# Three FFNs norm ahead of their products; 18 of 22 column tiles of w1 go in pairs by seven half-depth products

## The chip, the cores and the metric

One program runs on one core of one Trainium2 chip. The time is the device time of one execution in microseconds; before the change the median of three runs was 3161.38 us (3160.10 to 3161.64). The engines are named as in the profile: PE is TensorE, DVE VectorE, ACT ScalarE, POOL GpSimd, SP the queue that issues most DMAs.

## The reference

An encoder trunk of two layers for 512 prompt tokens and 32 sample tokens (544 together), width 1024, FFN width 2816. Only the FFNs are touched; `mixing` stands for a large projection, four branches and an output product.

```python
def rms_norm(x, g):
    y = x * lax.rsqrt(jnp.mean(x * x, axis=-1, keepdims=True) + EPS)
    return y * g
def swiglu(x, w1, w3, w2):
    return (jax.nn.silu(x @ w1) * (x @ w3)) @ w2
def layer(...):
    x = x + 0.5 * swiglu(rms_norm(x, n1), f1a, f1b, f1c)      # FFN1
    x = x + mixing(rms_norm(x, nm), ...)
    x = x + 0.5 * swiglu(rms_norm(x, n2), f2a, f2b, f2c)      # FFN2
    x = x + sigmoid(rms_norm(x, npl) @ wpg) * (p_i @ wpp)     # ple
```

All of it is in fp32.

## The kernel before

**Layout.** Activations lie with features on the partitions: `x` is eight tiles of 128 x 544. The tokens go in two halves `h` of 272 (`HT`). A product for one column tile of 128 weights and one half runs over the depth in steps of 128, and each step is three matmuls (`mm`, L344): the weight's high part with the activation's high part (`nh`, `ah`), high with the activation's low part (`nl`, `al`), low with the high part. High and low are two fp32r tiles which sum to the fp32 value.

**Weights.** The order of all products is planned ahead. `Weights.load` issues DMAs on SP into three raw tiles of 8 x 128 x 128; `split_next` casts the next job's raw tile to `hi` on ACT (L129) and leaves `lo = raw - hi` on DVE (L133) to be emitted after the cast of the next job (`late`, `finish`). Six tiles of each kind are live at most.

**Order.** The program is written as a sequence of units. `unit(fn)` splits one weight tile (`W.pump`), then emits the DVE work that earlier units put off (`settle` empties the list that `later` fills), then the unit itself, then a step of a side chain (`tick`). Each engine does its own list in that order; there is no scheduler. Products go to four PSUM banks in turn (`pm()`); four others serve statistics and side chains (`ps1()`).

**FFN.** `ffn` takes the 22 column tiles in parts of 8, 8 and 6 (`FF_PARTS`). For each tile f and half h, w1's product and w3's product are made; r is the token's factor rsqrt(mean(x^2)). DVE scales w1's product by r (`u`, L403), ACT makes tanh(u/2) (L297), DVE (tanh+1)*u (L306), w3's product times r (L403) and the product of both (L512), then ACT and DVE split it into `ah` (L323) and `al` (L321). After a part's tiles the d phase multiplies by w2 with the depth of that part and adds to x (L526), 16 units (m, h).

**Norms.** `Norm.update` runs as each x tile becomes final: hi and lo of x times gain (L370, L371), the square (L383), its sum on POOL. The two statistics matmuls (L392) stand inside the first unit of the next stage, behind its first product (`middle`), and r is applied to products only. `run_tail` emits the last product of the stage before. `p_chain` is a side chain for the per-layer embedding; it is started ahead of FFN2.

Of the kernel before, what the change touches and what calls it, by code (L numbers as in the profile page):

```python
# [27 lines left out]
FF_PARTS = ((0, 8), (8, 8), (16, 6))  # L28
OFF = dict(xp=0, q=512, k=1024, v=1536, gu=2048, gv=2560, lq=3072, lk=3328, lv=3584,
# [4 lines left out]
RAW_BUFS, W_BUFS, S_BUFS, T_BUFS = 3, 6, 57, 14  # L34
# [39 lines left out]
class Weights:  # L74

    def __init__(self, nc, raw_p, w_p):
        self.nc, self.raw_p, self.w_p = nc, raw_p, w_p
        self.chunks, self.jobs = [], []  # L80
        self.n_dma = self.n_split = self.live = 0
        self.raw_live = 0
        self.late = None

    def chunk(self, src, k0, nk, n0, ncols):

        step = max(1, 1024 // (nk * 128)) * 128
        hs = []
        for c in range(0, ncols, step):
            w = min(step, ncols - c)  # L90
            ck = dict(src=src, k0=k0, nk=nk, n0=n0 + c, n=w, left=1, raw=None, queued=False)
            job = dict(ck=ck, c=0, w=w, uses=2 * max(1, w // 128), hi=None, lo=None, queued=False)
            hs += [(job, o) for o in range(0, w, 128)]
        return hs

    def order(self, h):
        job = h[0]
        if not job["queued"]:
            job["queued"] = True
            self.jobs.append(job)  # L100
            if not job["ck"]["queued"]:
                job["ck"]["queued"] = True
                self.chunks.append(job["ck"])
# [10 lines left out]

    def split_next(self, lower=None):
        job = self.jobs[self.n_split]
        self.n_split += 1
        ck = job["ck"]
        while ck["raw"] is None:
            self.load()  # L120
        w = job["w"]
        if w < 128:
            both = self.w_p.tile([128, ck["nk"], 2 * w], F32R, tag="hi", name="hi")
            hi, lo = both[:, :, 0:w], both[:, :, w:2 * w]
        else:
            both = hi = self.w_p.tile([128, ck["nk"], w], F32R, tag="hi", name="hi")
            lo = self.w_p.tile([128, ck["nk"], w], F32R, tag="lo", name="lo")
# [14 lines left out]
        self.live += 1  # L142
# [7 lines left out]
    def pump(self, n=1):  # L150
        self.load()
        for _ in range(n):
            if self.n_split < len(self.jobs) and self.live < W_BUFS:
                self.split_next()

    def get(self, h):
        job, o = h
        while job["hi"] is None:
            assert self.live < W_BUFS, "weight slots"
# [13 lines left out]
def tile_encoder_step(ctx: ExitStack, tc: tile.TileContext, a, outs):  # L173
# [249 lines left out]
    for L in range(DEPTH):  # L423
        pl = {}

        def ffn_plan(key, w1, w3, w2):
            p1, p3, p2 = [], [], []
            for (f0, nf) in FF_PARTS:
                for f in range(f0, f0 + nf, 2):
                    c1 = W.chunk(w1, 0, 8, f * 128, 256)  # L430
                    c3 = W.chunk(w3, 0, 8, f * 128, 256)
                    p1 += c1
                    p3 += c3
# [22 lines left out]
        ffn_plan("ffn1", a["ffn1_w1"][L], a["ffn1_w3"][L], a["ffn1_w2"][L])  # L456
# [21 lines left out]
        ffn_plan("ffn2", a["ffn2_w1"][L], a["ffn2_w3"][L], a["ffn2_w2"][L])  # L478
# [1035 lines left out]
    with tc.manual_schedule():  # L1514
# [125 lines left out]
```

## Time and profile before

| what | value |
|---|---|
| median of three runs | 3161.38 us |
| the profiled execution | 3162.79 us |
| its span | 3160.8 us |
| mean granted clock of TensorE | 0.997 |
| PE busy | 3123.7 us, 99% |
| DVE busy | 1765.7 us, 56% |
| ACT busy | 1282.7 us, 41% |
| POOL busy | 312.3 us, 10% |

A busy engine is one with an instruction in it; matmuls overlap one another, so the mean length of one is more than the distance from one to the next. The chain of waits goes back from the last instruction to what released each step. The granted clock is a share of full speed: 1.00 is 2.4 GHz and 0.50 is 1.2 GHz.

### The profile page before, as it was taken

To read this page: it belongs to the slowest core of one execution; us is meant where nothing else is said; L and a number is where in the kernel's file an instruction comes from. 1 tells how busy PE (TensorE), PEld (TensorE's weight loads), DVE (VectorE), ACT (ScalarE), POOL (GpSimd) and SP (SyncE) were. 2 spreads that over 40 slices of the span, in tenths; PEclk is the share of its full clock that TensorE was granted. 3 is DMA by queue.
4 is the path that set the end of the run, shared out by engine and by line. 5 is a ranking of instruction groups with operands and counts; after the bars stand their busy time and mean duration, and the time that the engine had idled before them with its cause. 6 is when DMAs were issued, how large, how long until landed. Compare 5 with 4: busy or idle time off the path is not lost.

```text
span 3160.8 us, 58903 instructions
## 1 busy us (share of the span) xinstructions
PE 3123.7 (99%) x24756; PEld 3078.9 (97%) x24756; DVE 1765.7 (56%) x3503; ACT 1282.7 (41%) x2274; POOL 312.3 (10%) x413
## 2 busy tenths in 40 slices
PE   8999999999999999999999999999999999999999
PEld 8999998999999999999999999988999999999999
DVE  6444556866665554545654545477656645535454
ACT  4222334466664342223532223244666634323233
POOL 2000021201122000000300000112101211000010
PEclk9999999999999999999999999999999999999999
DMA  5333242224233323232323232422333232323221
GB/s 148 87 87 92 76 141 75 69 72 156 75 99 109 93 89 90 85 94 75 94 87 94 86 89 82 137 72 64 126 101 109 78 109 87 94 88 89 85 87 63
DMA packets 487337, 295.06 MB, mean 93 GB/s; under 512 B 13654, under 2 KB 472614, under 8 KB 487072
## 3 DMA queue, kind: packets, MB, share of 16 engines
q1 hardware_dynamic: 471392, 248.94, 27.1%
q0 software_dynamic: 11504, 34.55, 3.2%
q10 hardware_dynamic: 4176, 7.80, 0.7%
q8 instruction: 195, 3.19, 0.4%
q14 instruction: 70, 0.57, 0.1%
HBM read 270.41 MB, written 20.83 MB: 92 GB/s over the span
## 4 chain that ended last, share of the span: by engine, by line
PE 95%; DVE 3%; ACT 1%; issue 1%; DMA 0%; ACTq 0%; SPq 0%; DVEq 0%
PE pm L344 87%; DVE qe L828 1%; PE ps L868 1%; PE ps L1329 1%; PE ps L604 1%; PE ps L1320 1%; PE ps L1237 0%; PE ps L334 0%; DVE lo L133 0%; PE ps L1287 0%; PE ps L1286 0%; PE ps L905 0%; PE ps L1214 0%; PE ps L1176 0%; PE pm L707 0%
## 5 line engine op out<-in xcount | busy, mean ns | idle before, releaser
L344 PE MATMUL pm<-nh,hi 128*128 128x272 f32 x5248 | 1527.7, 291 | 0.0
L344 PE MATMUL pm<-nh,lo 128*128 128x272 f32 x5248 | 1512.2, 288 | 2.9 <-DVE lo L133 2.1
L344 PE MATMUL pm<-nl,hi 128*128 128x272 f32 x5248 | 1511.3, 288 | 0.0
L344 PEld LDWEIGHTS pm<-nh,hi 128*128 128x128 f32 x5248 | 989.4, 189 | 8.1 <-issue 5.9
L344 PEld LDWEIGHTS pm<-nh,lo 128*128 128x128 f32 x5248 | 988.1, 188 | 3.6 <-DVE lo L133 2.5
L344 PEld LDWEIGHTS pm<-nl,hi 128*128 128x128 f32 x5248 | 989.5, 189 | 1.2 <-DVE nl L1558 0.2
L129 ACT CAST hi<-raw 128x1024 fp32r<-128x1024 f32 (+2 forms) x478 | 491.0, 1027 | 390.2 <-PE pm L344 357.6
L133 DVE TENSOR_TENSOR lo<-raw,hi 128x1024 fp32r<-128x1024 f32 (+1 forms) x475 | 569.6, 1199 | 2.7 <-ACT hi L129 2.2
L403 DVE TENSOR_TENSOR u<-pm,r 128x272 f32<-128x272 f32 x560 | 246.4, 440 | 507.8 <-PE pm L344 497.7
L344 PE MATMUL pm<-ah,lo 128*128 128x272 f32 x1408 | 405.3, 288 | 0.0
L344 PE MATMUL pm<-al,hi 128*128 128x272 f32 x1408 | 405.2, 288 | 0.0
L344 PE MATMUL pm<-ah,hi 128*128 128x272 f32 x1408 | 405.2, 288 | 0.0
L344 PEld LDWEIGHTS pm<-al,hi 128*128 128x128 f32 x1408 | 265.0, 188 | 0.0
L344 PEld LDWEIGHTS pm<-ah,lo 128*128 128x128 f32 x1408 | 265.0, 188 | 0.0
L344 PEld LDWEIGHTS pm<-ah,hi 128*128 128x128 f32 x1408 | 264.9, 188 | 0.0
L323 ACT CAST ah<-sg 128x272 fp32r<-128x272 f32 x176 | 73.9, 420 | 439.9 <-DVE sg L512 439.9
L385 POOL TENSOR_TENSOR acc<-acc,sq 128x272 f32<-128x272 f32 x84 | 66.2, 789 | 1785.9 <-ACT sq L383 1785.9
L526 DVE SCALAR_TENSOR_TENSOR x<-pm,x 128x272 f32<-128x272 f32 x192 | 84.6, 441 | 270.3 <-PE pm L344 269.8
L297 ACT ACTIVATE sg<-u 128x272 f32<-128x272 f32 x192 | 82.9, 432 | 342.9 <-DVE u L403 342.9
L297 ACT ACTIVATE u<-u 128x272 f32<-128x272 f32 x160 | 69.0, 432 | 218.4 <-DVE u L403 218.2
L344 PE MATMUL pm<-yl,hi 128*128 128x272 f32 x512 | 147.4, 288 | 0.0
L344 PE MATMUL pm<-yh,hi 128*128 128x272 f32 x512 | 147.3, 288 | 0.0
(321 smaller groups left out, 3462.8 us busy)
## 6 DMA issues: line engine op xcount, KB each, us to landing
raw<-in_ffn_w_dram SPq DMA_DIRECT2D x240, 512.0 KB, 3.7
raw<-in_w_in_dram SPq DMA_DIRECT2D x136, 512.0 KB, 3.7
raw<-in_w_branch_dram SPq DMA_DIRECT2D x32, 512.0 KB, 3.4
raw<-in_ffn_w_dram SPq DMA_DIRECT2D x32, 384.0 KB, 3.1
raw<-in_w_out_dram SPq DMA_DIRECT2D x16, 512.0 KB, 3.6
raw<-in_ple_w_gate_dram SPq DMA_DIRECT2D x16, 512.0 KB, 3.5
yp<-park ACTq DMA_DIRECT2D x24, 272.0 KB, 4.5
park<-x POOLq DMA_DIRECT2D x16, 272.0 KB, 7.4
```

The lines of the kernel that those rows point to most:

```text
L129: self.nc.scalar.copy(hi, src)
L133: (lower or self.nc.vector).tensor_tensor(out=lo, in0=src, in1=hi.bitcast(F32), op=ALU.subtract)
L297: nc.scalar.activation(out, x, AF.Tanh, scale=scale)
L323: nc.scalar.copy(hi, src)
L344: nc.tensor.matmul(ps, lhsT=w[:, k, o:o + 128], rhs=x[:, hs(h)], start=first and k == 0 and j == 0, stop=last and k == n - 1 and j == 2)
L385: eng.tensor_tensor(out=self.acc[:, s], in0=self.acc[:, s], in1=q, op=ALU.add)
L403: nc.vector.tensor_tensor(out=out, in0=ps, in1=self.r[:, hs(h)], op=ALU.mult)
L526: nc.vector.scalar_tensor_tensor(out=x[m][:, hs(h)], in0=ps, scalar=0.25, in1=x[m][:, hs(h)], op0=ALU.mult, op1=ALU.add)
L604: nc.tensor.transpose(ps[0:n, g * 128:(g + 1) * 128], s[:, t0:t0 + n], ident)
L828: nc.vector.tensor_tensor(out=q2[r, e_].rearrange("p (b h) -> p b h", h=h), in0=uppers(e3[r, l], h), in1=uppers(qs, h), op=ALU.mult)
L868: nc.tensor.matmul(banks[f][0:n, j * n:(j + 1) * n], lhsT=kk, rhs=qq, start=True, stop=True)
L1320: nc.tensor.matmul(zb[n][:, 0:WID[n]], lhsT=ntri, rhs=sp[n][j][:, 0:WID[n]], start=j == 0, stop=False)
```

## The change

Three of the four FFNs (FFN2 of both layers and FFN1 of layer 1) get their input already normed (`PreNorm`) and run in `ffn7`; FFN1 of layer 0 stays. In `PreNorm` the statistics are taken at the end of the stage before; `normalise` makes y = x*r on DVE, hi = y*gain on ACT and lo on DVE for each x tile and half, and the FFN's products need no factor afterwards.

`ffn7` takes the tiles in parts of 4, 6, 6 and 6. The four tiles of part 0 go as plain products; in `first` three products are made together, step by step over the depth. In the other parts two tiles of w1 by two halves of tokens by two halves of depth are one 2 x 2 product of blocks (Winograd's form of Strassen): seven products of half the depth (12 matmuls each) in place of eight. Its operands are blocks and sums of blocks. Those of the weights (`a22, a11, s1, s3, a12, s2, s4`, `split_operand`) are summed in place in the raw tiles by DVE (L176 of the new kernel), cast by ACT (L179) and completed by DVE (L183); those of the activations (`t1` to `t4`) are made once per FFN by a side chain (`combine`). A pair's seven products, and four whole products of w3, are laid out in seven units (`pair`); products accumulate onto sums that DVE writes into PSUM.

Over the program 24182 matmuls become 23858: 27 pairs with 84 in place of 96. The w2 loads of the eight-deep and six-deep parts become four-deep and six-deep ones of the same bytes in all, 12 more DMAs; each FFN has 16 more updates of x. `p_chain` now starts ahead of the last part's d phase.

```diff
+QUAD = ("a22", "a11", "s1", "s3", "a12", "s2", "s4")
+FF_PARTS7 = ((0, 4), (4, 6), (10, 6), (16, 6))
...
+    def quad(self, src, n0):
+        c0, c1 = [dict(src=src, k0=0, nk=8, n0=n0 + c, n=128, left=1, raw=None, queued=False) for c in (0, 128)]
+        js = {name: dict(cks=[c0, c1] if name[0] == "s" else [(c0, c1)[int(name[1]) - 1]], of=(c0, c1), slots=1, uses=1,
+                         hi=None, lo=None, queued=False, kind=name) for name in QUAD}
+        return {name: (j, 0) for name, j in js.items()}
...
+    def split_operand(self, job):
+        name, (c0, c1) = job["kind"], job["of"]
+        both = self.slot(8, 128)
+        hi, lo = both[:, 0:4], both[:, 4:8]
+        v = self.nc.vector
+        a11, a12, a21, a22 = (c["raw"] and c["raw"][:, e::2, :] for c in (c0, c1) for e in (0, 1))
+        src, add = dict(a11=(a11, None), a12=(a12, None), a22=(a22, None), s1=(a22, a21), s3=(a21, a11),
+                        s2=(a11, a22), s4=(a12, a11))[name]
+        if add is not None:
+            v.tensor_tensor(out=src, in0=src, in1=add, op=ALU.add)
+            if name == "s2":
+                self.done_with(c1)
+        self.nc.scalar.copy(hi, src)
+        self.finish()
+        def low():
+            v.tensor_tensor(out=lo, in0=src, in1=hi.bitcast(F32), op=ALU.subtract)
+            if name == "s4":
+                self.done_with(c0)
+        self.late = (job, low)
+        job["hi"], job["lo"] = hi, lo
...
+    class PreNorm(Norm):
...
+        def normalise(self, h, ks):
+            s = hs(h)
+            low = None
+            for m in ks:
+                if self.out[m] is None:
+                    self.out[m] = (st(f"nh{m}", F32R), st(f"nl{m}", F32R))
+                if self.y[h][m // 2] is None:
+                    self.y[h][m // 2] = st("y")
+                hi, lo = (p[:, s] for p in self.out[m])
+                y, g = self.y[h][m // 2][:, hs(m % 2)], self.gain[:, m:m + 1]
+                nc.vector.tensor_tensor(out=y, in0=self.x[m][:, s], in1=self.r[:, s], op=ALU.mult)
+                nc.scalar.mul(hi, y, g)
+                if low:
+                    low()
+                def low(hi=hi, lo=lo, y=y, g=g):
+                    nc.vector.scalar_tensor_tensor(out=lo, in0=y, scalar=g, in1=hi.bitcast(F32),
+                                                   op0=ALU.mult, op1=ALU.subtract)
+            low()
...
+        def combine(self):
+            self.minus = lay.tile([128, 8], F32, tag="minus", name="minus")
+            nc.vector.tensor_scalar(self.minus, self.gain, -1.0, None, op0=ALU.mult)
+            for j in range(4):
+                g, g2, m2 = self.gain[:, 2 * j:2 * j + 1], self.gain[:, 2 * j + 1:2 * j + 2], \
+                    self.minus[:, 2 * j + 1:2 * j + 2]
+                y1, y2 = self.y[0][j], self.y[1][j]
+                self.y[0][j] = self.y[1][j] = None
+                d = st("yd")
+                nc.vector.tensor_tensor(out=d, in0=y1, in1=y2, op=ALU.subtract)
+                (ha, la), (hb, lb) = self.sums[j] = [(st("sh", F32R), st("sl", F32R)) for _ in range(2)]
+                sa, sb = st("sa"), st("sb")
+                t1 = sa[:, 0:HT]
+                nc.scalar.mul(t1, d[:, 0:HT], g)
+                b12 = tt_("b12")
+                nc.scalar.mul(b12, y2[:, 0:HT], g)
+                yield
...
+                b22 = y2[:, HT:T]
+                stt = nc.vector.scalar_tensor_tensor
+                stt(out=sa[:, HT:T], in0=b22, scalar=m2, in1=t1, op0=ALU.mult, op1=ALU.subtract)
+                nc.scalar.copy(ha, sa)
+                stt(out=sb[:, 0:HT], in0=b22, scalar=g2, in1=b12, op0=ALU.mult, op1=ALU.subtract)
+                stt(out=sb[:, HT:T], in0=d[:, HT:T], scalar=m2, in1=t1, op0=ALU.mult, op1=ALU.add)
+                nc.scalar.copy(hb, sb)
+                yield
...
+        if isinstance(norm, PreNorm):
+            for m, h in order[:-1]:
+                unit(lambda: fn(m, h))
+                if (m, h) == (7, 0):
+                    later(norm.finish)
+            norm.stats(0)
+            W.pump(1)
+            settle()
+            norm.normalise(0, range(0, 2))
+            fn(*order[-1])
+            norm.normalise(0, range(2, 4))
+            norm.finish()
+            tick(1)
+            norm.normalise(0, range(4, 8))
+            return
...
+                    c3 = W.chunk(w3, 0, 8, f * 128, 256)
+                    p3 += c3
+                    if parts is FF_PARTS7 and f0 > 0:
+                        q = W.quad(w1, f * 128)
+                        p1 += [q, None]
+                        for x in [q[n] for n in QUAD[:-1]] + [c3[0], q["s4"], c3[1]]:
+                            W.order(x)
+                        continue
...
+        def other(f, h, t, sign=1.0):
+            ps = pm()
+            mm(ps, p3[f], norm.out, h)
+            later(lambda: half_done(f, h, t, ps, sign))
...
+        def first(h):
+            tiles = [pm(), pm(), pm()]
+            ws = [W.get(x) for x in (p1[0], p3[0], p1[1])]
...
+                if k == 3 and h == 0:
+                    norm.stats(1)
+            for x in (p1[0], p3[0], p1[1]):
+                W.used(x)
+            t = silu(tiles[0])
+            t2 = silu(tiles[2])
+            later(lambda: half_done(0, h, t, tiles[1]))
+            return t2
...
+        def product(ps, w, b, first=True):
+            hi, lo, _ = W.get(w)
+            for j, (xh, xl) in enumerate(norm.block(b)):
+                for i, (u, z) in enumerate(((hi, xh), (hi, xl), (lo, xh))):
+                    nc.tensor.matmul(ps, lhsT=u[:, j, :], rhs=z, start=first and j == 0 and i == 0,
+                                     stop=j == 3 and i == 2, skip_group_check=not first)
+            W.used(w)
...
+            def u1():
+                v["a"], v["e"], v["b"] = pm(), pm(), pm()
+                product(v["a"], q["a11"], "b11")
+                product(v["e"], q["s1"], "t1")
+                product(v["b"], q["s2"], "t2")
+                v["as"], v["es"] = tt_("as"), tt_("es")
+                nc.scalar.copy(v["as"], v["a"])
+                nc.scalar.copy(v["es"], v["e"])
+                def sums():
+                    nc.vector.tensor_tensor(out=v["b"], in0=v["b"], in1=v["as"], op=ALU.add)
+                    nc.vector.tensor_tensor(out=v["e"], in0=v["b"], in1=v["es"], op=ALU.add)
+                later(sums)
+            def u3():
+                product(v["a"], q["a12"], "b21", first=False)
+                v["t11"] = silu(v["a"])
+                later(lambda: half_done(f, 0, v["t11"], v["g"]))
+                product(v["b"], q["s3"], "t3", first=False)
+                product(v["e"], q["s4"], "b22", first=False)
+                def last_one():
+                    c = v["es"]
+                    nc.vector.tensor_tensor(out=c, in0=v["b"], in1=c, op=ALU.add)
+                    v["t22"] = silu(c, -1.0)
+                later(last_one)
+                v["t12"] = silu(v["e"])
+            def u2():
+                v["g"] = pm()
+                mm(v["g"], p3[f], norm.out, 0)
+            def u5():
+                product(v["b"], q["a22"], "t4", first=False)
+                v["t21"] = silu(v["b"], -1.0)
+            unit(u1)
+            unit(u2, pump=2)
+            unit(u3)
+            unit(lambda: other(f, 1, v["t12"]), pump=2)
+            unit(u5)
+            unit(lambda: other(f + 1, 0, v["t21"], -1.0))
+            unit(lambda: other(f + 1, 1, v["t22"], -1.0))
...
+            if part == 0:
+                for h in (0, 1):
+                    settle()
+                    t2 = first(h)
+                    unit(lambda: other(1, h, t2), pump=0)
+                    if h == 0:
+                        norm.normalise(1, range(8))
+                c_sums = start(norm.combine(), front=True)
+                for f in range(2, nf):
+                    for h in (0, 1):
+                        def f_unit():
+                            ps = pm()
+                            mm(ps, p1[f], norm.out, h)
+                            t = silu(ps)
+                            W.pump(1)
+                            other(f, h, t)
+                        unit(f_unit)
+            else:
+                if part == 1:
+                    drain(c_sums)
+                for f in range(f0, f0 + nf, 2):
+                    pair(f)
...
-            ffn(pl["ffn1"], x, norm, nm)
-            n2 = Norm(x, v["norm_ffn2"])
+            (ffn7 if L else ffn)(pl["ffn1"], x, norm, nm)
+            n2 = PreNorm(x, v["norm_ffn2"])
             mixing(L, v, x, nm, n2)
             npl = Norm(x, v["norm_ple"])
             ppair.clear()
-            start(p_chain(L))
-            ffn(pl["ffn2"], x, n2, npl)
+            ffn7(pl["ffn2"], x, n2, npl, p_chain(L))
...
-                norm = Norm(x, vn["norm_ffn1"])
+                norm = PreNorm(x, vn["norm_ffn1"])
```

**A pair's fourth unit.** On ACT, in the first pair of FFN2 of layer 0 (the new kernel), the rows from the cast of `s1` of the next pair (w_14068) on; pm_13990 is the bank `a`, pm_13991 the bank `e`, w_14112 is `s3` of the next pair:

```order
L179 CAST w_14068<-raw_13926 128x512
L343 ACTIVATE sg_14084<-pm_13990 128x272
L343 ACTIVATE sg_14110<-pm_13991 128x272
L179 CAST w_14112<-raw_13926 128x512
L179 CAST w_14116<-raw_13988 128x512
L369 CAST ah_14120<-sg_14084 128x272
L343 ACTIVATE sg_14125<-es_14030 128x272
```

On DVE in the same place:

```order
L176 TENSOR_TENSOR raw_13926<-raw_13926,raw_13988 128x4x128
L183 TENSOR_TENSOR w_14068<-raw_13926,w_14068 128x512
L183 TENSOR_TENSOR w_14112<-raw_13926,w_14112 128x512
L352 SCALAR_TENSOR_TENSOR sg_14084<-sg_14084,pm_13990 128x272
L708 TENSOR_TENSOR sg_14084<-sg_14084,pm_14043 128x272
L778 TENSOR_TENSOR es_14030<-pm_13992,es_14030 128x272
```

and on PE, the last product of the third unit and the first matmuls of the fourth, whose bank pm_14128 is the one that pm_13990 had:

```order
L747 MATMUL pm_13991<-nh5_13104,w_13922 128x272
L747 MATMUL pm_13991<-nh7_13115,w_13922 128x272
L747 MATMUL pm_13991<-nl7_13116,w_13922 128x272
L747 MATMUL pm_13991<-nh7_13115,w_13922 128x272
L390 MATMUL pm_14128<-nh0_13048,hi_13862 128x272
L390 MATMUL pm_14128<-nl0_13049,hi_13862 128x272
```

In the kernel before, on DVE at the end of part 0 of the same FFN, the same steps read:

```order
L321 TENSOR_TENSOR al_15668<-sg_15641,ah_15667 128x272
L403 TENSOR_TENSOR u_15700<-pm_15674,r_13151 128x272
L133 TENSOR_TENSOR lo_15607<-raw_15478,hi_15606 128x1024
L306 SCALAR_TENSOR_TENSOR sg_15702<-sg_15702,u_15700 128x272
L403 TENSOR_TENSOR u_15700<-pm_15675,r_13151 128x272
L512 TENSOR_TENSOR sg_15702<-sg_15702,u_15700 128x272
L133 TENSOR_TENSOR lo_15705<-raw_15576,hi_15704 128x1024
```

DVE's read of the bank (there L403, here L352) stood ahead of the weight tile's lo that the same unit cast; now it stands behind the lo of `s3`, whose cast stands on ACT behind the tanh of `e`.

**Part 0's d phase.** On DVE, in the new kernel's FFN2 of layer 0, around the first two updates of x (L832); al_13611 is the low part of tile 3:

```order
L367 TENSOR_TENSOR al_13611<-sg_13567,ah_13610 128x272
L352 SCALAR_TENSOR_TENSOR sg_13639<-sg_13639,pm_13614 128x272
L708 TENSOR_TENSOR sg_13639<-sg_13639,pm_13646 128x272
L832 SCALAR_TENSOR_TENSOR x_12545<-pm_13689,x_12545 128x272
L525 SCALAR_TENSOR_TENSOR sa_13677<-y_13241,minus_13444,sa_13677 128x272
L527 SCALAR_TENSOR_TENSOR sb_13678<-y_13241,norm_ffn2_274,b12_13680 128x272
L528 SCALAR_TENSOR_TENSOR sb_13678<-yd_13671,minus_13444,sa_13677 128x272
L176 TENSOR_TENSOR raw_13573<-raw_13573 128x4x128
L183 TENSOR_TENSOR w_13682<-raw_13606,w_13682 128x512
L367 TENSOR_TENSOR al_13611<-sg_13639,ah_13610 128x272
L832 SCALAR_TENSOR_TENSOR x_12545<-pm_13713,x_12545 128x272
```

and before:

```order
L133 TENSOR_TENSOR lo_15705<-raw_15576,hi_15704 128x1024
L321 TENSOR_TENSOR al_15668<-sg_15702,ah_15667 128x272
L526 SCALAR_TENSOR_TENSOR x_12545<-pm_15745,x_12545 128x272
L526 SCALAR_TENSOR_TENSOR x_12545<-pm_15771,x_12545 128x272
L133 TENSOR_TENSOR lo_15739<-raw_15610,hi_15738 128x1024
L526 SCALAR_TENSOR_TENSOR x_12547<-pm_15803,x_12547 128x272
```

The low part of the last tile's second half (L367, before L321) now stands behind an update of x, three steps of `combine` (L525, L527, L528), a weight sum and a lo; before it stood ahead of the updates.

**From mixing into FFN2.** On ACT, at the end of layer 0's mixing, in the new kernel (L374 and L375 make r, L157 casts a weight tile, L496 makes hi of the normed input):

```order
L467 ACTIVATE sq_13004<-x_12559 128x272
L429 ACTIVATE sq_13033<-x_12557 128x272
L334 ACT_TABLE_LOAD
L374 ACTIVATE r_13036<-ps_13037,eps_94 128x272
L375 ACTIVATE r_13036<-r_13036 128x272
L157 CAST hi_13042<-raw_12883 128x1024
L496 ACTIVATE nh0_13048<-y_13050,norm_ffn2_274 128x272
L496 ACTIVATE nh1_13053<-y_13050,norm_ffn2_274 128x272
```

and before (L328 and L329 make r):

```order
L129 CAST hi_13118<-raw_12982 128x1024
L288 ACT_TABLE_LOAD
L328 ACTIVATE r_13151<-ps_13152,eps_94 128x272
L329 ACTIVATE r_13151<-r_13151 128x272
L328 ACTIVATE r_13151<-ps_13157,eps_94 128x272
L329 ACTIVATE r_13151<-r_13151 128x272
L297 ACT_TABLE_LOAD
L297 ACTIVATE sg_13163<-u_13161 128x272
```

Before, the products' inputs were ready ahead of r; now hi of the first x tile comes behind the table load, both steps of r and a weight tile's cast.

## Rows read from the trace of the kernel before

**Rows 1.** The page's busy times by engine and the granted clock in 40 slices.

```profile
PE 3123.7 (99%) x24756; PEld 3078.9 (97%) x24756; DVE 1765.7 (56%) x3503; ACT 1282.7 (41%) x2274; POOL 312.3 (10%) x413
```

**Rows 2.** The chain that ended last: shares of the span by engine, and by line.

```profile
PE 95%; DVE 3%; ACT 1%; issue 1%; DMA 0%; ACTq 0%; SPq 0%; DVEq 0%
PE pm L344 87%; DVE qe L828 1%; PE ps L868 1%; PE ps L1329 1%; PE ps L604 1%; PE ps L1320 1%; PE ps L1237 0%; PE ps L334 0%; DVE lo L133 0%; PE ps L1287 0%; PE ps L1286 0%; PE ps L905 0%; PE ps L1214 0%; PE ps L1176 0%; PE pm L707 0%
```

**Rows 3.** Pieces of that chain in order of time (start, length, what): the seam ahead of layer 1's FFN1, and that FFN's matmuls.

```profile
1589.42 0.92 PE ps L392 x4
1590.34 397.28 PE pm L344 x3168
```

**Rows 4.** Busy time in the stretch of layer 1's FFN1: start:end, length, PE, PEld, DVE, ACT, POOL (number of instructions), granted clock, DMA share, GB/s.

```profile
1590.00:1988.00 398.00, 398.00 (x3173) 397.88 (x3172) 200.05 (x357) 120.55 (x196) 12.94 (x18) 1.00 0.31 89
```

**Rows 5.** Groups of instructions of one shape: total busy us, mean ns of one, idle before.

```profile
L133 DVE TENSOR_TENSOR lo<-raw,hi 128x1024 fp32r<-128x1024 f32 x443 | 539.2, 1217 | 2.7 <-ACT hi L129 2.2
...
L129 ACT CAST hi<-raw 128x1024 fp32r<-128x1024 f32 x444 | 464.1, 1045 | 390.1 <-PE pm L344 357.6 <-DMA raw<-in_w_in_dram 24.9 <-PE pm L707 6.1
...
L526 DVE SCALAR_TENSOR_TENSOR x<-pm,x 128x272 f32<-128x272 f32 x192 | 84.6, 441 | 270.3 <-PE pm L344 269.8
...
L297 ACT ACTIVATE sg<-u 128x272 f32<-128x272 f32 x192 | 82.9, 432 | 342.9 <-DVE u L403 342.9
...
L306 DVE SCALAR_TENSOR_TENSOR sg<-sg,u 128x272 f32<-128x272 f32 x176 | 77.2, 439 | 48.6 <-ACT sg L297 48.6
...
L288 ACT ACT_TABLE_LOAD x32 | 41.1, 1283 | 5.1 <-issue 4.0 <-PEq L1625 0.7
...
L383 ACT ACTIVATE sq<-x 128x272 f32<-128x272 f32 x98 | 40.7, 415 | 0.0
...
L371 DVE SCALAR_TENSOR_TENSOR nl<-x,norm_ffn,nh 128x272 fp32r<-128x272 f32 x48 | 34.3, 715 | 11.9 <-ACT nh L370 11.3 <-DMA sb_k_norm<-in_sb_k_norm_dram 0.6
...
L328 ACT ACTIVATE r<-ps,eps 128x272 f32<-128x272 f32 x62 | 29.8, 481 | 10.9 <-PE ps L334 6.6 <-PE ps L392 4.1
...
L370 ACT ACTIVATE nh<-x,norm_ffn 128x272 fp32r<-128x272 f32 x48 | 25.1, 523 | 67.6 <-DVE x L1438 49.3 <-DVE x L1456 15.7 <-issue 2.5
...
L321 DVE TENSOR_TENSOR spo<-spl,sph 128x512 fp32r<-128x512 f32 x32 | 21.8, 722 | 9.5 <-ACT sph L323 9.5
...
L1332 DVE TENSOR_TENSOR aw<-aw,ps 128x512 f32<-128x512 f32 x32 | 20.5, 683 | 18.7 <-PE ps L1329 18.7
...
L323 ACT CAST sph<-spl 128x512 fp32r<-128x512 f32 x32 | 18.1, 611 | 2.9 <-issue 2.9
```

**Rows 6.** Timeline (start, length, engine, line, operation): the last matmul of a product and the DVE update that reads it, and the last step of r.

```profile
1125.62 0.29 PE L344 MATMUL pm<-mh,lo 128*128 128x272 f32 x1
1125.95 0.44 DVE L1438 SCALAR_TENSOR_TENSOR x<-pm,x 128x272 f32<-128x272 f32 x1 [0.49 <-PE pm L344]
...
1591.28 0.43 ACT L329 ACTIVATE r<-r 128x272 f32<-128x272 f32 x1
```

**Rows 7.** Timeline: PE's instructions that came behind a wait of 1.6 to 2.7 us, with the wait in brackets and what ended it.

```profile
526.31 0.33 PE L849 MATMUL ps<-ident,ke 128*128 128x128 f32 x1 [2.61 <-POOL ke L819]
603.50 0.49 PE L868 MATMUL ps<-qe,ke 128*128 128x128 f32 x2 [1.62 <-DVE sg L1015]
638.01 0.60 PE L334 MATMUL ps<-sql,bd 128*128 128x272 f32 x1 [2.68 <-DVE sql L321]
2090.77 0.33 PE L849 MATMUL ps<-ident,ke 128*128 128x128 f32 x1 [2.62 <-POOL ke L819]
2165.27 0.49 PE L868 MATMUL ps<-qe,ke 128*128 128x128 f32 x2 [1.60 <-DVE sg L1015]
2199.78 0.40 PE L334 MATMUL ps<-sql,bd 128*128 128x272 f32 x1 [2.67 <-DVE sql L321]
3133.88 0.39 PE L344 MATMUL pm<-nh,lo 128*128 128x272 f32 x1 [1.69 <-DVE lo L133]
```

**Rows 8.** Busy time in stretches of 4 us around and behind those waits (columns as in rows 4).

```profile
524.00:528.00 4.00, 1.43 (x11) 1.27 (x12) 3.94 (x13) 0.85 (x3) 2.25 (x2) 1.00 0.48 131
528.00:532.00 4.00, 4.00 (x35) 3.96 (x33) 3.32 (x12) 2.17 (x6) 0.00 (x0) 1.00 0.01 4
636.00:640.00 4.00, 1.99 (x9) 1.99 (x10) 3.10 (x8) 2.45 (x5) 0.00 (x0) 0.72 0.28 77
640.00:644.00 4.00, 4.00 (x31) 4.00 (x31) 2.32 (x9) 1.71 (x4) 0.00 (x0) 0.85 0.18 55
2088.00:2092.00 4.00, 1.13 (x8) 0.81 (x7) 3.96 (x11) 1.31 (x3) 2.72 (x2) 0.98 0.47 131
2092.00:2096.00 4.00, 4.00 (x23) 4.00 (x23) 3.36 (x14) 1.87 (x5) 0.00 (x0) 0.59 0.00 0
2200.00:2204.00 4.00, 4.00 (x24) 4.00 (x24) 1.52 (x5) 3.31 (x6) 0.00 (x0) 0.63 0.45 131
2204.00:2208.00 4.00, 4.00 (x41) 3.54 (x39) 2.80 (x12) 0.68 (x2) 0.00 (x0) 0.94 0.00 0
604.00:608.00 4.00, 4.00 (x34) 3.84 (x34) 3.34 (x13) 1.64 (x3) 0.58 (x1) 1.00 0.17 70
2168.00:2172.00 4.00, 4.00 (x42) 3.70 (x42) 3.86 (x13) 0.44 (x1) 0.22 (x1) 1.00 0.07 25
```

More of the change, by code (lines that the diff above doesn't have):

```diff
@@ L100, in order @@
             self.jobs.append(job)
-            if not job["ck"]["queued"]:
-                job["ck"]["queued"] = True
-                self.chunks.append(job["ck"])
+            for ck in job["cks"]:
+                if not ck["queued"]:
+                    ck["queued"] = True
+                    self.chunks.append(ck)
     def load(self):
@@ L113, in load, with done_with, slot @@
             self.n_dma += 1
+    def done_with(self, ck):
+        ck["left"] -= 1
+        if ck["left"] == 0:
+            ck["raw"] = False
+            self.raw_live -= 1
+        self.load()
+    def slot(self, nk, w, name="w"):
+        return self.w_p.tile([128, nk, w], F32R, tag="w", name=name)
     def split_next(self, lower=None):
@@ L152, in pump @@
         for _ in range(n):
-            if self.n_split < len(self.jobs) and self.live < W_BUFS:
+            if self.n_split < len(self.jobs) and self.live + self.jobs[self.n_split]["slots"] <= W_BUFS:
                 self.split_next()
@@ L158, in get @@
         while job["hi"] is None:
-            assert self.live < W_BUFS, "weight slots"
+            assert self.live + self.jobs[self.n_split]["slots"] <= W_BUFS, "weight slots"
             self.split_next()
@@ L403, in scale_to, with __init__, update, finish @@
             nc.vector.tensor_tensor(out=out, in0=ps, in1=self.r[:, hs(h)], op=ALU.mult)
+    class PreNorm(Norm):
+        def __init__(self, x, gain):
+            super().__init__(x, gain)
+            self.y = [[None] * 4, [None] * 4]
+            self.last = None
+            self.sums = [None] * 4
+        def update(self, m, h):
+            s = hs(h)
+            if m < 7:
+                self.square(m, s)
+                return
+            q = tt_("sq")
+            nc.scalar.square(q, self.x[m][:, s])
+            self.last = lambda: nc.vector.tensor_tensor(out=self.acc[:, s], in0=self.acc[:, s], in1=q, op=ALU.add)
+        def finish(self):
+            f, self.last = self.last, None
+            f()
+        def stats(self, h):
+            if self.r is None:
+                self.r = st("r")
+            assert side["free"] > 0
+            ps = ps1()
+            nc.tensor.matmul(ps[:, 0:HT], lhsT=m1024, rhs=self.acc[:, hs(h)], start=True, stop=True)
+            rsqrt_of(ps[:, 0:HT], self.r[:, hs(h)])
+            rel()
+            if h == 1:
+                self.acc = None
+        def normalise(self, h, ks):
+            s = hs(h)
+            low = None
[39 more added lines that the diff above has]
+                yield
+                for h_, l_, s_ in ((ha, la, sa), (hb, lb, sb)):
+                    nc.vector.tensor_tensor(out=l_, in0=s_, in1=h_.bitcast(F32), op=ALU.subtract)
+                yield
+        def block(self, name):
+            if name[0] == "b":
+                m0, s = {"b11": (0, 0), "b21": (1, 0), "b22": (1, 1)}[name]
+                return [[p[:, hs(s)] for p in self.out[2 * j + m0]] for j in range(4)]
+            i = int(name[1]) - 1
+            return [[p[:, hs(i % 2)] for p in self.sums[j][i // 2]] for j in range(4)]
```

86 lines of the change are left out of this document (65 added, 21 removed).

## The prediction, made before the changed kernel ran

> **What bounds the kernel now.** I read the busy times first: PE is busy 99% of the span, DVE 56%, ACT 41% [rows 1]. The chain of waits says the same: PE holds 95% of it, the matmuls of line 344 alone 87% [rows 2]. In order of time, layer 1's FFN1 is one piece of 397.28 us with 3168 matmuls and no wait in it, and the seam ahead of it costs 0.92 us, the time of its statistics matmuls [rows 3]. In that stretch DVE is busy 200.05 of 398.00 us and ACT 120.55 [rows 4]. So an FFN ends with PE, and a matmul costs 397.28 / 3168 = 0.1254 us. A matmul taken away is worth that as long as PE still never waits; any wait that PE gets is paid whole.
>
> **What it removes.** 27 pairs lose 12 matmuls each: 324 x 0.1254 = 40.6 us. This is the ceiling. Per FFN DVE also loses the scaling by r, which lay beside PE and was worth nothing.
>
> **What it adds beside PE.** A pair has 84 matmuls of half depth and 96 of w3: 180 x 0.1254 = 22.6 us. DVE does in it seven lows of 512 elements (0.722), four sums of 512 (priced as the 0.683 of line 1332), two lows of 1024 (1.217) and some fifteen operations of 272 (0.44): 5.1 + 2.7 + 2.4 + 6.6 = 16.8 us [rows 5]. ACT does seven casts of 0.611, two of 1.045, two copies, four tanhs and four casts of some 0.43: 10.7 us [rows 5]. Both fit on average, so the bulk is hidden; if not, DVE would have to grow by a third. The 12 further DMAs carry no more bytes, and `p_chain`'s transfers start earlier than they are needed: I set both at nothing, with a bound of 2 us each way.
>
> **Where PE waits: the pair's fourth unit.** The order shows it. The fourth unit's product goes to the bank of `a`, which is free when DVE's line 352 has read it. That stands on DVE behind the low of `s3` of the next pair, that behind its cast on ACT, the cast behind the tanh of `e`, and the tanh behind the very last matmul ahead of the unit. So from the moment at which PE could go on: 0.20 until a reader starts (a matmul's row ends 0.16 after the next one's start, 0.29 less 0.125; the reader starts 0.04 later [rows 6]), tanh 0.432, cast 0.611, low 0.722, line 352 0.439, and 0.04 at each of the hand-overs: 2.45 to 2.55 us, of which nothing overlaps. In the third pair of a part the tile pumped there is one of w2, whose cast does not come behind `e`'s tanh in this way, and I count no wait. 18 pairs x 2.45 = 44 us. Bounds: 2.2 to 2.7 a pair where it happens as the order says (40 to 49), and 0 where ACT or DVE are early in a way I do not see.
>
> **Part 0's d phase.** Its units are 12 matmuls, 1.5 us. Counting from the last w3 product, the low of the last tile's second half is done only after DVE's multiplication, an update of x that itself waits for the first d product (at 1.5 + 0.20), three steps of `combine`, a sum, a low and the low itself: 1.7 + 4 x 0.44 + 0.683 + 0.722 + 0.44 = 5.3 [rows 5]. PE needs it for the eleventh matmul of the second unit, at 1.5 + 1.25 = 2.75. It waits 2.6 us. From the second update of x to the ninth DVE then has some 16 us (seven updates, the rest of `combine` with six lows of 544 elements, sums and lows of weights), and PE has 10.5 for the same units; four banks buffer 4.5 of that, so about 1.3 more is waited. 4 us in each FFN2; in layer 1's FFN1 fewer of these rows stand ahead of the low, some 3.5 in all. Sum 12, bounds 3 x 2 and 3 x 7.
>
> **Seams.** What was 0.92 us [rows 3] becomes a chain. Mixing to FFN2, counted from the end of the product ahead of the statistics: 0.20, update 0.44, square 0.415, table load 1.283, r in 0.481 and 0.43 [rows 5, 6], a weight cast of 1.045, hi of the first tile 0.523 [rows 5] and hand-overs: 4.9. PE has one product and a statistics matmul meanwhile, 3.0 + 0.46. It waits 1.4. Then every depth step of `first` has 9 matmuls (1.13 us) and DVE has y and a low for it (0.44 + 0.715), squares and an update beside them, so some 0.9 more is lost, and 0.7 ahead of the second half: 3 us, twice. From ple to FFN1 the same chain has the gate's steps in it: 1.1 for the first tile; 1.2 because the third product's bank is read by a DVE step behind two lows; 1.3 because ACT loads tanh's table again and x's last update stands ahead of the next y; and in the unit behind `first` 3.4, since a weight's low (1.217) stands behind tanhs and line 352. 7 us. Sum 13, bounds 6 and 18.
>
> **Clock.** The trace of before has four waits of PE of 2.61 to 2.68 us and three of 1.60 to 1.69 [rows 7]. Behind three of the four the granted clock fell in the stretches of 4 us that follow: 0.72 and 0.85; 0.98 and 0.59; 0.63 and 0.94. Each time that is (1 - clock) x 4 summed, about 1.7 us lost. Behind the fourth, at 526.31, it stayed 1.00, as it did behind those of 1.60 and 1.62 [rows 8]. The pair's wait of some 2.3 us of idle lies between. I let half of the 18 fall: 9 x 1.7 = 16 us, and one or two more at d phases and seams: 18 in all. Bounds 0 and 35.
>
> The Trainium skill (TensorE: Matmul & The Clock Gate, section "Why this matters for your kernels") speaks against such a change: it asks for no idle gaps between bursts of matmuls in the middle of a kernel, as these give back the clock. The gap that it names is longer than every wait of rows 7, so by it alone none of the new waits would cost clock and the sum would be that of rival B below; rows 8 show falls behind shorter waits, and I follow the rows.
>
> **Sum.** -40.6 + 44 + 12 + 13 + 18 = +46 us on the profiled execution's 3162.79, or 3209. The median of the runs is 1.4 us below that execution: 3208.
>
> **Rivals.** (A) PE does not wait in the pairs: the order on ACT and DVE holds, but a bank or a row that I read as the same is another, or only a part of the 2.45 is idle. Then -40.6 + 12 + 13, with one or two us of clock: about 3148. For it speaks that DVE and ACT have room on average [rows 4], against it that the four rows in question are in one line behind PE's last matmul, and PE's next stands behind them. (B) The waits come as worked out, but none is long enough to bring down the clock: 28 us, 3190. The three waits of 1.6 to 1.7 without a fall speak for it [rows 7, 8]. (C) Nearly every pair's wait brings the clock down (31 us, and 4 at the other places), and the pair's wait is 2.7: 3229. Three falls of four behind waits 0.3 us longer speak for it. (D) The gain is there but the waits eat just as much: half the pairs wait, no clock, 3146 + 22 = 3168, near no change.
>
> **Chances.** My forecast 0.52, B 0.23, C 0.13, A 0.07, D 0.05. About 0.2%, 6.3 us, is what a measurement of this kernel can tell from no change. Faster than that comes from A alone, 0.07; within it from half of D and a little of A, 0.04; slower 0.89. The forecast's own range is 3195 to 3222; to hold 8 in 10 with B and most of C it goes from 3172 to 3236.
>
> **What would show it.** In the profile of the changed kernel PE's waits by what ended them should have line 352 of the new kernel as the largest entry, some 18 times about 2.3 us, and the chain should take ACT's tanh and cast and DVE's low just there. The low of line 367 should end three waits near 2.6 us at the first d phases, and lines 496 and 501 those at the seams. The FFN's number of matmuls is 3060 in place of 3168; its length, if I am right, is 397 - 13.5 + 15 + 4 + 3 to 7 + 6. The granted clock's row should show dips in the pair stretches, by three stretches per FFN. I am wrong if line 352 ends fewer than ten waits, if the clock stays 1.00 in every FFN, or if PE waits in the pairs for weight tiles or transfers.

## The result, and the profile after

The changed kernel took 3206.57 us (median of four runs, 3206.03 to 3207.27), the kernel before 3161.51; the ratio is 1.0140, with a 95% interval of 1.0125 to 1.0155. It is slower by 45 us; 3208 was forecast, in a range of 3172 to 3236.

The span of the profiled execution went from 3160.8 to 3205.5 us. The first view is the chain of the changed kernel, its shares by engine and by line, which answers to [rows 2]. Line 390 is `mm` (344 before), 747 the pair's product, 732 `first`:

```profile
PE 92%; DVE 5%; ACT 2%; issue 1%; DMA 0%; SPq 0%; ACTq 0%; DVEq 0%
PE pm L390 74%; PE pm L747 9%; PE pm L732 1%; DVE qe L1135 1%; PE ps L1636 1%; PE ps L1175 1%; PE ps L911 1%; PE ps L1627 1%; DVE w L183 1%; PE ps L1544 0%; DVE lo L161 0%; PE ps L380 0%; ACT w L179 0%; PE ps L1594 0%; PE ps L1593 0%
```

PE gave up 3% of the chain, and besides the two products two names are new among the lines: DVE's low of a pair's weight operand (183) and ACT's cast for it (179). The trace counts 24432 matmuls in place of 24756, 324 fewer, as planned. Next, what PE waited for: engine, line, what it waited for; us in total, times, the longest.

```profile
PE pm L390 <- DVE sg L352: 37.2, 18, 2.1
...
PE pm L390 <- DVE lo L161: 6.5, 4, 2.7
PE pm L390 <- DVE al L367: 5.6, 3, 2.1
...
PE pm L732 <- ACT nh L496: 4.6, 5, 1.2
...
PE pm L390 <- ACT hi L157: 1.4, 1, 1.4
```

Of all these only one wait of 1.69 us on a weight's low was there before, near the end [rows 7]. The 18 on line 352 are the read of the bank of `a`. The chain around the first of them, in order of time (start, length, what), and behind the dots what followed another of them, the one that ended at 1356.06:

```profile
1212.98 3.01 PE pm L747 x24
1215.99 0.02 issue
1216.01 0.40 ACT sg L343
1216.41 0.52 ACT w L179
1216.92 0.02 issue
1216.95 0.69 DVE w L183
1217.64 0.36 DVE sg L352
1218.00 0.04 issue
1218.04 4.80 PE pm L390 x24
...
1356.06 3.27 PE pm L390 x24
```

This is the row that the prediction drew from the order alone: PE's product ends, then tanh, cast, low, read, and PE goes on. The last two lines show something more: 24 matmuls took 4.80 us behind this wait, 3.27 behind the other, and 3.01 where PE had not stopped before (the first line). So 0.26 us goes to PE's start after a stop. The other 1.53 is half-clock, as the stretches behind the two waits show (start:end, length, PE, PEld, DVE, ACT, POOL, granted clock, DMA share, GB/s):

```profile
1216.00:1220.00 4.00, 1.96 (x9) 1.96 (x10) 2.95 (x7) 2.34 (x6) 0.00 (x0) 0.79 0.00 0
1220.00:1224.00 4.00, 4.00 (x28) 4.00 (x27) 2.26 (x6) 0.90 (x2) 0.00 (x0) 0.78 0.45 131
1356.00:1360.00 4.00, 3.94 (x31) 3.94 (x32) 3.68 (x10) 1.57 (x4) 0.00 (x0) 1.00 0.20 58
1360.00:1364.00 4.00, 4.00 (x34) 4.00 (x33) 3.07 (x6) 2.21 (x4) 0.00 (x0) 1.00 0.25 75
```

Both waits are 2.07 us; behind the first the clock fell (0.79 and 0.78 are means over 1.00 and 0.50), behind the second it did not. Read in this way behind each of the 18, it fell 13 times. By the granted clock, (1 - clock) x 4 summed, each fall is 1.70 to 1.72 us. In time it costs 1.5: from one pair to the next it is 24.9 us without a fall and 26.4 with one. At half-clock a matmul follows the one before it after 0.227 us in place of 0.125, which is less than twice as long.

Last the three FFNs as stretches, from the end of the stage ahead to the end of their own. After, and then before:

```profile
1124.68:1538.39 413.71, 397.89 (x3077) 394.97 (x3075) 242.31 (x452) 161.02 (x298) 11.56 (x15) 0.98 0.29 86
1599.76:2018.71 418.95, 396.29 (x3066) 392.27 (x3065) 242.22 (x453) 162.15 (x296) 9.36 (x12) 0.98 0.29 84
2722.49:3132.98 410.49, 394.69 (x3077) 391.78 (x3076) 242.18 (x452) 161.15 (x298) 11.46 (x15) 0.98 0.30 87
```

```profile
1125.76:1525.15 399.39, 399.39 (x3184) 398.81 (x3183) 200.17 (x356) 123.14 (x201) 10.72 (x15) 1.00 0.30 89
1586.25:1984.44 398.19, 398.19 (x3174) 398.03 (x3173) 200.42 (x356) 121.52 (x197) 9.38 (x12) 1.00 0.31 88
2688.24:3088.20 399.96, 399.96 (x3182) 399.39 (x3182) 200.14 (x356) 123.16 (x201) 10.57 (x14) 1.00 0.30 89
```

The three grew by 14.3, 20.8 and 10.5 us, 45.6 in all, and the span by 44.7: the whole loss is here. DVE is still under 60% busy in them, and yet PE stands still for 16 to 23 us of each (length less PE's busy time); before it stood still for none.

### The profile page after: what moved, and what is told of

Same layout as the page of the kernel before. It is cut to its first block, busy times and chain, and to the rows that moved or that the text cites. A ratio compares the mean times of both kernels' runs of the same rounds, so it can differ in the third digit from the quotient of the medians.

```text
span 3205.5 us, 58756 instructions
## 1 busy us (share of the span) xinstructions
PE 3118.7 (97%) x24432; PEld 3065.9 (96%) x24432; DVE 1861.7 (58%) x3746; ACT 1383.1 (43%) x2525; POOL 320.2 (10%) x413
## 4 chain that ended last, share of the span: by engine, by line
PE 92%; DVE 5%; ACT 2%; issue 1%; DMA 0%; SPq 0%; ACTq 0%; DVEq 0%
PE pm L390 74%; PE pm L747 9%; PE pm L732 1%; DVE qe L1135 1%; PE ps L1636 1%; PE ps L1175 1%; PE ps L911 1%; PE ps L1627 1%; DVE w L183 1%; PE ps L1544 0%; DVE lo L161 0%; PE ps L380 0%; ACT w L179 0%; PE ps L1594 0%; PE ps L1593 0%
## 5 line engine op out<-in xcount | busy, mean ns | idle before, releaser
L390 PE MATMUL pm<-nh,hi 128*128 128x272 f32 x4240 | 1249.3, 295 | 38.6 <-DVE sg L352 37.2
L390 PE MATMUL pm<-nh,lo 128*128 128x272 f32 x4240 | 1232.5, 291 | 6.5 <-DVE lo L161 6.5
L390 PE MATMUL pm<-nl,hi 128*128 128x272 f32 x4240 | 1232.2, 291 | 0.0
L390 PEld LDWEIGHTS pm<-nh,hi 128*128 128x128 f32 x4240 | 809.6, 191 | 50.6 <-DVE sg L352 41.1
L390 PEld LDWEIGHTS pm<-nh,lo 128*128 128x128 f32 x4240 | 809.4, 191 | 7.6 <-DVE lo L161 7.4
L390 PEld LDWEIGHTS pm<-nl,hi 128*128 128x128 f32 x4240 | 810.4, 191 | 0.9
L157 ACT CAST hi<-raw 128x1024 fp32r<-128x1024 f32 (+1 forms) x434 | 434.8, 1005 | 132.6 <-PE pm L390 74.8
L449 DVE TENSOR_TENSOR u<-pm,r 128x272 f32<-128x272 f32 x296 | 130.1, 440 | 224.0 <-PE pm L390 217.7
L183 DVE TENSOR_TENSOR w<-raw,w 128x512 fp32r<-128x512 f32 x189 | 129.7, 686 | 125.6 <-ACT w L179 125.6
L179 ACT CAST w<-raw 128x512 fp32r<-128x512 f32 x189 | 114.2, 620 | 201.7 <-DVE raw L176 139.2
L747 PE MATMUL pm<-sh,w 128*128 128x272 f32 x864 | 176.4, 289 | 0.0
L832 DVE SCALAR_TENSOR_TENSOR x<-pm,x 128x272 f32<-128x272 f32 x192 | 83.7, 439 | 132.1 <-PE pm L390 131.6
```

The lines of the kernel that those rows point to most:

```text
L157: self.nc.scalar.copy(hi, src)
L179: self.nc.scalar.copy(hi, src)
L183: v.tensor_tensor(out=lo, in0=src, in1=hi.bitcast(F32), op=ALU.subtract)
L390: nc.tensor.matmul(ps, lhsT=w[:, k, o:o + 128], rhs=x[:, hs(h)], start=first and k == 0 and j == 0, stop=last and k == n - 1 and j == 2)
L449: nc.vector.tensor_tensor(out=out, in0=ps, in1=self.r[:, hs(h)], op=ALU.mult)
L747: nc.tensor.matmul(ps, lhsT=u[:, j, :], rhs=z, start=first and j == 0 and i == 0, stop=j == 3 and i == 2, skip_group_check=not first)
```

## The experiments

Each run was timed in three rounds beside the kernel before. Times are medians.

**The read of the bank put first.** In `pair`:

```diff
             unit(u3)
+            settle()
             unit(lambda: other(f, 1, v["t12"]), pump=2)
```

> The fourth unit of a pair emits DVE's deferred work (with the read of bank a, line 352) before it splits the next weight operands, so that this read no longer stands behind the cast and the low of s3. Theory: each of the 18 waits cost 2.07 us of idle and 0.25 of refill, and 13 of them a clock fall of 1.7; all of it goes: 3206.6 - 18 x 2.32 - 13 x 1.7 = 3143, and no wait on line 352 is left. Rival (DVE has too much to do in the unit, the order is only where it shows): the wait turns up in the next units, the time stays within 10 us of 3207.

Measured: 3145.76 us, ratio 0.9948 (0.9933 to 0.9963). No wait on line 352 is left, and none came in its place; all other waits are the ones listed above, to the tenth. In the stretch with the first part's three pairs PE never stops:

```profile
1210.00:1280.00 70.00, 70.00 (x561) 70.00 (x560) 40.94 (x77) 27.64 (x52) 0.00 (x0) 1.00 0.31 91
```

So 61 us hung on where a few DVE instructions stand; 18 x (2.07 + 0.26) + 13 x 1.5 is 61 too. DVE's amount of work is the same, and it has room; the rival falls.

**A shorter wait.**

```diff
             unit(u3)
+            late[:] = late[-1:] + late[:-1]
+            settle()
             unit(lambda: other(f, 1, v["t12"]), pump=2)
```

> As the run before, but with DVE's read of bank e put ahead of its read of bank a: PE's next unit then waits for the tanh of e and two reads, without cast and low, about 1.3 us in place of 2.07. It tells whether the clock's fall hangs on the length of the wait. Theory (short waits bring no fall, as the waits of 1.6 us before the change): 18 x 0.77 less idle and none of the 13 falls: 3206.6 - 13.9 - 22.1 = 3171, with the clock at 1.00 in the pairs. Rival (the falls come from the pair's pattern of products, not from the wait's length): about 13 falls remain, 3193.

Measured: 3179.42 us, ratio 1.0053 (1.0038 to 1.0067). The waits were shorter than expected, and there were more of them, since the third pair of a part has this one too:

```profile
PE pm L390 <- DVE sg L352: 25.9, 27, 1.0
```

27 of 0.96 us, and behind none of them did the clock fall. From one pair to the next it is 23.76 us in this run and 22.54 in the run before: a wait of 0.96 costs 1.22, so here too 0.26 goes to PE's start after a stop. 27 x 1.22 = 33 is the distance from 3145.8 to 3179.4, within 1 us. On the clock the theory holds: no falls with the same products and more stops.

**A longer wait.**

```diff
             unit(u3)
-            unit(lambda: other(f, 1, v["t12"]), pump=2)
+            if not ends:
+                W.pump(2)
+                W.finish()
+            unit(lambda: other(f, 1, v["t12"]), pump=2 if ends else 0)
```

(`ends` is set for the third pair of a part.)

> The wait is made longer: the low of a12 too is emitted ahead of the read of bank a, one more low of 0.69 us, so 2.76 in place of 2.07, in the same 18 pairs. Theory: 18 x 0.69 = 12.4 more idle, and all 18 waits bring the clock down in place of 13, 8.5 more: 3228. Rival (falls do not hang on the length): 13 falls as now, 3219.

Measured: 3225.84 us, ratio 1.0201 (1.0186 to 1.0217). The 18 waits are 2.67 us each:

```profile
PE pm L390 <- DVE sg L352: 48.0, 18, 2.7
```

The clock fell behind 16 of them, once for twice as long. 48.0 - 37.2 = 10.8 us is idle, and 4 more lengths of fall at 1.5 are 6; the sum, 16.8, is near the 15.6 by which the profiled span grew (3205.5 to 3221.1). That execution was the fastest of four, which go from 3222.90 to 3228.38; the medians are 19.3 apart. The time lies between the two expectations (3228 and 3219), nearer to the theory's.

**Without the pairs.**

```diff
-                    if parts is FF_PARTS7 and f0 > 0:
+                    if False:
...
-                c_sums = start(norm.combine(), front=True)
-                for f in range(2, nf):
+                norm.y = None
+            if True:
+                for f in range(f0 if part else 2, f0 + nf):
...
-            else:
-                if part == 1:
-                    drain(c_sums)
-                for f in range(f0, f0 + nf, 2):
-                    pair(f)
```

> All the rest of the change without the pairs: the three FFNs are normed ahead and go in parts of 4, 6, 6, 6, but every tile of w1 is a plain product, and no sums are made. It gives the price of the seams and the four-tile part by themselves. Theory: 3206.6 + 40.6 (324 matmuls) - 41.8 - 22.1 (the pairs' waits and falls) = 3183, less up to 5 because part 0's d phase no longer has the sums on DVE: 3178 to 3183. Rival (the seams and the d phase are hidden, all of the loss is the pairs'): 3162.

Measured: 3181.04 us, ratio 1.0061 (1.0044 to 1.0077). The norms ahead and the part of four tiles cost 19.5 us over 3161.5. On top of that the pairs cost 25.5 as they were ordered, and win 35.3 with the read put first (3181.0 to 3145.8), of the 40.6 that their matmuls are worth. Here the waits on line 367 are 1.5 us in place of 5.6, since no sums stand on DVE in the d phase; these 4.1 us are most of what 35.3 lacks.

**Part 0's d phase.**

```diff
+                if part == 0:
+                    settle()
+                    settle()
                 for m in range(8):
```

> Only part 0's d phase is changed: the deferred work of the last tile is emitted in full ahead of the first update of x, so the low of its second half no longer stands behind that update and the three steps of the sums. Theory: the three waits on line 367 (5.6 us, 0.25 of refill each) and one clock fall of 1.7 go: 3206.6 - 8 = 3198. Rival (DVE has more work than PE in this phase, as the prediction had it, so PE waits a unit or two later for a bank): 3 us at most are won, 3204, and waits on line 832 come instead.

Measured: 3203.89 us, ratio 1.0130 (1.0114 to 1.0147). The rival holds. The wait's row, and a stretch of the FFN2 of layer 0 in which PE waits (columns as above):

```profile
PE pm L390 <- DVE x L832: 4.0, 7, 1.1
...
1190.00:1195.00 5.00, 4.20 (x34) 3.98 (x33) 4.76 (x11) 3.03 (x6) 0.00 (x0) 1.00 0.37 108
```

The 5.6 us on line 367 are gone, and seven waits for the updates of x came; they had been 0.4 us, once. DVE is busy 4.76 of 5.00 us there, 19.35 of the 20 from 1180 on, and falls behind PE; taking out the first wait lets the next one show.

**FFN1 of layer 1 in its old form.**

```diff
-        ffn_plan("ffn1", a["ffn1_w1"][L], a["ffn1_w3"][L], a["ffn1_w2"][L], FF_PARTS if L == 0 else FF_PARTS7)
+        ffn_plan("ffn1", a["ffn1_w1"][L], a["ffn1_w3"][L], a["ffn1_w2"][L], FF_PARTS)
...
-            (ffn7 if L else ffn)(pl["ffn1"], x, norm, nm)
+            ffn(pl["ffn1"], x, norm, nm)
...
-                norm = PreNorm(x, vn["norm_ffn1"])
+                norm = Norm(x, vn["norm_ffn1"])
```

> FFN1 of layer 1 is given back its old form; the two FFN2 keep the new one. Theory: each FFN's loss is its own, and layer 1's FFN1 lost 20.8 us (its stage went from 398.2 to 418.9): 3186, and the two FFN2 keep their 12 waits on line 352. Rival (the loss is shared with the stages around, and comes back elsewhere): 3195 or more.

Measured: 3184.49 us, ratio 1.0070 (1.0055 to 1.0085): 22.1 less, where its stage had grown by 20.8. The twelve waits on line 352 in the two FFN2 stayed (24.8 us). Each FFN's loss is its own.

**The seams.**

```diff
             norm.stats(0)
-            W.pump(1)
             settle()
             norm.normalise(0, range(0, 2))
+            W.pump(1)
...
             norm.normalise(0, range(4, 8))
+            W.finish()
             return
...
-                    unit(lambda: other(1, h, t2), pump=0)
+                    unit(lambda: other(1, h, t2), pump=h)
```

> Only the seams are changed: the weight's cast stands behind the hi of the first two x tiles, the weight's low is emitted with the norm, and the next tile is split one unit earlier. Theory: of the 10.9 us of PE's waits at the seams some 7 go, with 0.25 of refill for three of them, and one clock fall: 3206.6 - 9.5 = 3197. Rival (DVE, which makes the normed tiles, sets the pace there, and the cast and the low only stand in its shadow): under 3 us, 3204.

Measured: 3199.75 us, ratio 1.0119 (1.0104 to 1.0134), so 6.8 won: between the two, nearer to the theory. The four runs go from 3197.03 to 3203.08. The waits on a weight's hi or low at the seams are gone, those on the norm itself stayed, and one on line 449 is new:

```profile
PE pm L733 <- ACT nh L496: 4.4, 7, 0.8
PE pm L390 <- DVE lo L161: 1.7, 1, 1.7
PE pm L733 <- DVE u L449: 1.1, 1, 1.1
```

The 1.7 is the one that was there before the change. 4.4 us of the norm's own chain are left. The 1.1 on line 449 is the edit's own: DVE's read of a bank for the gate of ple now stands behind the weight's low (1.22 us), and the third product of `first` waits for that bank. One wait on line 367 grew, 1.48 to 2.08 in layer 1's FFN1.

**The three edits together.**

> The three edits together: the pairs' read of bank a first (3145.8 alone), the low ahead of part 0's d phase, the seams. Theory: the waits are separate and add up: 3145.8 - 6.4 - 7.8 and one or two falls of 1.7 at the seams: 3128 to 3131, 1.0% under the kernel before. Rival (waits taken out at one place come back at the next): 3140.

Measured: 3136.36 us, ratio 0.9918 (0.9903 to 0.9933). The single edits won 60.8, 2.7 and 6.8, which from 3206.6 makes 3136.3: within the spread of the seam run the places are separate and their prices add up. The expectation was lower (3128 to 3131) because it had 6.4 for the d phase, which by itself wins 2.7, and more for the seams. This version beats both kernels; 0.8% is 26 us against the kernel before.

**The sums' lows on POOL.** In the version with all three edits:

```diff
                 for h_, l_, s_ in ((ha, la, sa), (hb, lb, sb)):
-                    nc.vector.tensor_tensor(out=l_, in0=s_, in1=h_.bitcast(F32), op=ALU.subtract)
+                    nc.gpsimd.tensor_tensor(out=l_, in0=s_, in1=h_.bitcast(F32), op=ALU.subtract)
```

> The three edits together as in the run before (3136.4), and the lows of the activations' sums made on POOL in place of DVE, which takes 8 x 0.717 = 5.7 us from DVE in each part-0 d phase. It tells whether the 3.4 us of waits on the updates of x (line 834) there are DVE having too much to do. Theory: they go, with 0.25 of refill for each of six: 3136.4 - 4.9 = 3131. Rival (the waits come from the order of updates and sums, not from the amount; or POOL's slower lows hold up the first pair): no gain, 3136 or more.

Measured: 3138.17 us, ratio 0.9927 (0.9910 to 0.9943): no gain. The waits on line 834 (the update of x) went from 3.4 to 5.8 us. The timeline of layer 0's FFN2 shows why (start, length, engine, line, operation):

```profile
1186.95 1.88 POOL L532 TENSOR_TENSOR sl<-sa,sh 128x544 fp32r<-128x544 f32 x1 [3.38 <-ACT sh L526]
1187.54 0.43 DVE L834 SCALAR_TENSOR_TENSOR x<-pm,x 128x272 f32<-128x272 f32 x1
1187.89 1.49 DVE L176 TENSOR_TENSOR raw<-raw 128x512 f32<-128x512 f32 x1
1188.80 1.79 POOL L532 TENSOR_TENSOR sl<-sb,sh 128x544 fp32r<-128x544 f32 x1
1189.31 1.82 DVE L183 TENSOR_TENSOR w<-raw,w 128x512 fp32r<-128x512 f32 x1
```

Beside POOL's operation DVE's sum took 1.49 and its low 1.82, each ending 0.55 after POOL's, while both take 0.68 by themselves; the update of x, which reads PSUM, took its usual 0.43. So the work was taken off DVE's list, and DVE's time was not. Whether the amount of work or its order makes the d phase's waits this run doesn't tell.

## Why the prediction was right

The direction, the size and the main cause were those of the prediction. Its terms against what was measured:

| term | forecast | measured |
|---|---|---|
| 324 matmuls | -40.6 | held: a pair that does not wait takes 22.54, its 180 matmuls at 0.1254 are 22.57; -35.3 with the sums' cost in it |
| pairs' waits | 44 | 18 x (2.07 + 0.26) = 42 |
| d phases | 12 | 5.6 + 0.4 idle, 0.26 x 4: 7 |
| seams | 13 | 10.8 idle (6.5 - 1.7 + 4.6 + 1.4), 0.26 x 9: 13 |
| clock | 18 | 15 falls of 1.5 in the three FFNs: 23 |
| sum | 46 | 44 with -40.6 in the first row, where the three stretches grew by 45.6 |

**The pairs' waits** came at the 18 places that the order gave, and the third pair had none. The chain was 2.05 and not 2.45 long: a cast took 0.52 in it, not 0.611, DVE's steps 0.69 and 0.36. PE's slow start, 0.26, nearly makes up for that; the prediction had it in the 0.20 at the beginning.

**The d phases** were mis-sized. "It waits 2.6 us" was 2.07 and 2.08 in the two FFN2, and 1.48 in layer 1's FFN1; but the step that failed is the "1.3 more" for the work that DVE has left, added on top (and 16 less 10.5 and 4.5 is 1.0). While PE waits for the low, DVE gets on with that work; only when the first wait is taken out does the second show, 4.0 in place of 5.6. Two waits that come from one backlog are not added.

**The seams** came out at the forecast's sum, by two errors: mixing to FFN2 cost about 1.3 us of idle each and not 3, ple to FFN1 8.3 and not 7. The first matmul there waits 1.15 us for the norm's hi; what was said of 9 matmuls a step against DVE's pace cost hardly anything. Of the lines named as a sign, 496 ended waits of 4.6 us and 501 none; a weight's low and hi (161, 157) ended 6.2.

**The clock** was the term with the widest bounds and is the one that was too low: half of the 18 was taken (9 x 1.7, which is 15 and not 16), 13 fell, and two more at a d phase and a seam; each cost 1.5 and not 1.7. The reading of [rows 8] behind it stopped too early. The stretches behind the wait at 526.31 end at 532; the clock did fall from 535.4 on, to 0.50 in 536:540, and for twice as long as at the three falls that were read. What PE had done just before were three waits of 0.38, 0.52 and 1.20 us within 4 us. In the changed kernel the same wait of 2.61 brought the clock down at once, 0.68 and 0.50 in the two stretches from 524. So "three of four" was a count of chances, and had to be read as such. The two errors, 5 us too many in the d phases and 5 too few here, cancel; that the median was met within 2 us is partly luck.

**The terms set at nothing**, the 12 further DMAs and `p_chain`, stayed there: in the three FFNs no wait of PE ended with a transfer.

**The rivals.** A (PE does not wait) and D (half of the pairs wait) fell with the first profile. B (no fall at such waits) fell with the 13. C (nearly every wait) is what the longer wait made of it. The Trainium skill (TensorE: Matmul & The Clock Gate, section "Why this matters for your kernels") warns of idle gaps longer than any wait of the pairs; here a wait of 2.07 in the pairs cost clock in two cases of three, so the measurement decides against reading that length as a safe bound.

## What to carry to other kernels

Before fewer matmuls are bought with more operations on other engines, look in the order for the one instruction that frees PE's next bank, and at what stands ahead of it on its engine: 61 us hung on emitting the deferred reads of PSUM ahead of the next weight operand, on a DVE that was busy under 60%. A stop of PE costs its length and a quarter of a microsecond, and in these pairs, at some 2 us, in two cases of three 1.5 more by the clock. Waits at separate places add up, waits of one backlog do not.

## What the runs showed of the hardware

**Longer waits brought the clock down more often, but length alone does not settle it.** In the pairs it fell behind 0 of 27 waits of 0.96 us; 45 of 66 of 2.06 or 2.07 (13 of 18 in the changed kernel, 12 of 18, 8 of 12 and 12 of 18 in the runs on the d phase, FFN2 and the seams); 16 of 18 of 2.67. Which of the 2.07 fall differs from kernel to kernel, the number hardly. Elsewhere the counts are others: of 13 waits of 2.06 to 2.08 on line 367, ahead of a d phase's matmuls, in six traces 3 brought a fall; and three waits of 1.39, 1.42 and 0.74 within 7 us, at the seam ahead of layer 1's FFN1, brought one in each of the six traces that have them. One fall costs 1.5 us. What decides in a single case no run here shows.

**DVE stands still beside POOL** when both read two tiles of SBUF: 0.68 became 1.49 and 1.82. The Trainium skill (SBUF — State Buffer, section "Who interferes with whom") says that a DVE instruction with two inputs in SBUF contends with a GpSimd instruction that reads SBUF for a shared port, which is locked exclusively, and that DVE with at most one such input does not; the trace agrees, with the 0.43 of the update from PSUM beside it. Whether DVE holds up POOL as well these rows do not show.
